# A hybrid decoder layer on one core: reciprocal roots on a few rows instead of whole tiles, the last block's second scale inside the feed-forward stage, S5 operators fetched a step sooner, the sample softmax placed later

## The chip, the cores and the metric

One NeuronCore of a Trainium2 chip runs the whole program: TensorE (PE, with its weight loads shown apart as PEld), VectorE (DVE), ScalarE (ACT), GpSimd (POOL), and one queue of SyncE (SP) from which every DMA is issued. The metric is device microseconds for one execution, median of several runs; less is better.

## The reference

One inference step of one decoder layer (width 1024) for a prompt of 2048 tokens and for 8 single-token samples that share all weights. Cut to what matters:

```python
h = rmsnorm(x)
[u_ssm | u_pool | q_mem | gate_logits] = h @ w_in
o_ssm  = S5 state-space branch of u_ssm, GELU, GLU
o_pool = trailing means of u_pool (windows 2,4,8,16), mapped per group, scaled
o_mem  = 4-head cross-attention from q_mem into 256 memory tokens
merged = sum_b sigmoid(gate_b) * (o_b @ w_branch_up[b])
x = x + rmsnorm(merged @ w_out)
x = x + rmsnorm(SwiGLU(rmsnorm(x)))
# rmsnorm(x) = x * rsqrt(mean(x*x) + eps) * g, in float32
```

The samples attend into caches of their own: 8 samples x 4 heads x 256 keys of 128, read from HBM.

## The kernel before

All tensors lie transposed, channels on the partitions and tokens on the free axis. Float32 accuracy comes from splitting every operand into a high part (ACT, L171) and a rest (DVE or POOL, L172) and adding three matmuls, hi*hi, hi*lo and lo*hi (`mmk`, L117). Those into the six PSUM tiles `pa` are called main matmuls here; transposes (L120) and small products go to the two tiles `pb`.

The prompt is cut into four blocks q = 0 to 3 of 512 tokens; block 1 (`QS`) carries the 8 samples too and is 520 wide, cut into 256 and 264. The mix stage runs over the blocks: `ssm_project`, `projections` and `gates` for the three branches in the order of a table, `out_project`, and `residual`. Then comes the feed-forward stage in two halves (`ffn_in`, with Strassen's seven products over sums of block pairs that `sums` computes and stores in `d_S`, loaded as tiles `S`) and `ffn_out`.

Work that is not main matmuls is written as generators in a list `background`; main code calls `step()` between its matmuls and so draws one piece of the list at a time, and `flush()` draws all that is left. The compiler's scheduler then fixes one order of instructions for each engine. Every engine executes its own order strictly, so a matmul that waits holds all matmuls behind it, and a DMA issue on SP that waits for a free buffer holds all issues behind it. `yield` is the place where a generator hands back; an empty `yield` pushes the rest of it one piece later.

The pieces that the change touches:

- A scale. `rsqrt_mean` sums squares over channels with one matmul against a tile of ones (every partition of the result holds the same row of 512 sums), and then computes 1/sqrt by a bit trick and three Newton steps on the full 128 x 512 tile: 11 DVE operations (L354, L342, L343, three times L345 to L347). It is used 11 times: `norm_stats` (blocks 1 to 3) and twice in each `residual`.
- `rsqrt_quick` (already used elsewhere: first norm, memory norm, finish) puts the sums into 4 columns of 128 tokens (5 of 104 in block 1) with matmuls of one column (`pb<-ones,tmp` in the trace), does the same steps on 128 x 4 (12 DVE operations, L367 to L373), and spreads the result back: one DVE multiply of the identity per column (L380), one 128-wide matmul against ones per column (`pb<-tmp,ones`), one ACT copy (L390).
- `residual(q)`: first scale; for each of 8 channel tiles a DVE multiply (L1253), a POOL add (L1254), a store, an ACT square (L1257), a DVE add into `st2` (L1259); then the second scale from `st2`, stored to `d_rb2`, which only `sums` reads. `residual(3)` runs alone, after all mix work and before the feed-forward stage.
- `s5_group(q, g)`: per block four groups. Operators `op(0..6)` are loaded from `d_ops` (L798) into six buffers `ops`; `op(2..4)` serve the matmuls of its last step.
- `sample_attention` (in block 1): per sample a broadcast load of the query (L1102), two loads of keys (L1106), POOL multiplies (L1107) and DVE reductions to scores `sc` (L1108), all through four buffers `xr`; two PE transposes of `sc` (L1110) start the softmax; its result goes to `d_ps`, and 16 steps with the values follow the same way (L1127 to L1132).

Of the kernel before, what the change touches and what calls it, by code (L numbers as in the profile page):

```python
# [13 lines left out]
I32 = mybir.dt.int32  # L14
# [3 lines left out]
MUL, ADD, SUB = ALU.mult, ALU.add, ALU.subtract  # L18
# [110 lines left out]
def trunk(ctx, tc, nc, I, O):  # L129
# [7 lines left out]
            "ev": 4, "S": 56, "f": 52, "z": 8}  # L137
    SIZE = {"tmp": 528, "ops": 512, "G": 512, "wr": 1024, "wh": 1024, "wl": 1024, "wt": 1024,
            "ev": HW_, "S": HW_, "f": HW_, "z": HW_}
    COMMON = ("xr", "tmp", "rb", "wr", "wh", "wl")  # L140
    stage = [None]

    def nm(tag):
# [3 lines left out]
    def slot(tag, dt=F32):  # L147
        n = nm(tag)
        p = base if tag in COMMON else stage[0]
        return p.tile([P, SIZE.get(tag, W520)], dt, tag=tag, name=n, bufs=BUFS[tag])  # L150
# [9 lines left out]
    def psum2():  # L160
        n = nm("pb")
        return psp.tile([P, 512], F32, tag="pb", name=n, bufs=2)
# [11 lines left out]
    def blocks(q):  # L174
        return [(0, 256), (256, 264)] if q == QS else [(0, 512)]

    def width(q):
        return W520 if q == QS else TQ
# [158 lines left out]
    def each(q, ps):  # L337
        return [(p_[:, :n], slice(o, o + n)) for p_, (o, n) in zip(ps, blocks(q))]

    def rsqrt_core(d, v, n):  # L340
        a = slot("tmp")[:, :n]
        V.tensor_scalar(d.bitcast(I32), v.bitcast(I32), -0.5, float(0x5F3759DF), MUL, ADD)  # L342
        V.tensor_scalar(v, v, -0.5, None, MUL)  # L343
        for _ in range(3):
            V.tensor_tensor(a, d, d, MUL)  # L345
            V.tensor_tensor(a, a, v, MUL)
            V.scalar_tensor_tensor(d, a, 1.5, d, ADD, MUL)  # L347

    def rsqrt_mean(dst, sums, bl):
        v = slot("tmp")  # L350
        for o, n in bl:
            ps = psum2()
            T.matmul(ps[:, :n], lhsT=ones, rhs=sums[:, o:o + n], start=True, stop=True)
            V.tensor_scalar(v[:, o:o + n], ps[:, :n], 1.0 / DM, EPS, MUL, ADD)  # L354
        sl = slice(bl[0][0], bl[-1][0] + bl[-1][1])
        rsqrt_core(dst[:, sl], v[:, sl], sl.stop - sl.start)

    def rsqrt_rows(sums, bl):
        lo, hi = bl[0][0], bl[-1][0] + bl[-1][1]
        ns = next(i for i in range(-(-(hi - lo) // P), 99) if (hi - lo) % i == 0)  # L360
# [31 lines left out]
    def rsqrt_quick(dst, sums, bl):  # L392
        rows = rsqrt_rows(sums, bl)
        spread(rows, bl[0][0], dst)
        return rows
# [35 lines left out]
    def norm_stats(q):  # L431
        n = width(q)
        st = slot("tmp")
        for k in range(KD):
            xt = load_x(q, k)
            if k == 0:
                S.activation(st[:, :n], xt[:, :n], AF.Square)
            else:
                sq = slot("tmp")
                S.activation(sq[:, :n], xt[:, :n], AF.Square)  # L440
                G.tensor_tensor(st[:, :n], st[:, :n], sq[:, :n], ADD)
            if k % 2:
                yield
        rb = slot("rb")
        rsqrt_mean(rb, st, blocks(q))
        nc.sync.dma_start(d_rb[q, :, :n], rb[:, :n])
        yield

# [346 lines left out]
    def s5_group(q, g, U, us, out):  # L795
        def op(i):
            t = slot("ops")
            nc.sync.dma_start(t, d_ops[g, i])  # L798
            return t

        Bre, Bim = op(0), op(1)
        pu = psum2()
        for i in range(4):
            T.transpose(pu[:, i * P:(i + 1) * P], U[:, i * P:(i + 1) * P], ident)
        Ut = slot("U")
        S.activation(Ut[:, :512], pu, AF.Copy)
        yield
        e = []
        for B in (Bre, Bim):
            pe = psum2()  # L810
            for i in range(4):
                sl = slice(i * P, (i + 1) * P)
                T.matmul(pe[:, sl], lhsT=B[:, sl], rhs=Ut[:, sl], start=True, stop=True)
            e.append(pe)
        if q == QS:
            samp = sample_state(g, us, Bre, Bim)
        Cs, Sn = op(5), op(6)
        Gr, Gi = slot("G"), slot("G")
        gr, gi = Gr[:, :512], Gi[:, :512]
        t0, t1 = slot("tmp")[:, :512], slot("tmp")[:, :512]  # L820
        V.tensor_tensor(gr, Cs, e[0], MUL)
        V.tensor_tensor(t1, Sn, e[0], MUL)
        V.tensor_tensor(t0, Sn, e[1], MUL)
        V.tensor_tensor(gi, Cs, e[1], MUL)
        G.tensor_tensor(gr, gr, t0, ADD)
        G.tensor_tensor(gi, gi, t1, SUB)
        yield
        for i in range(4):
            r = 4 * g + i
            sl = slice(i * P, (i + 1) * P)  # L830
            dec = r4[:, r:r + 1].to_broadcast([P, P])
            V.tensor_tensor_scan(gr[:, sl], dec, gr[:, sl], carry[0][:, r:r + 1], MUL, ADD)
            V.tensor_tensor_scan(gi[:, sl], dec, gi[:, sl], carry[1][:, r:r + 1], MUL, ADD)
        yield
        t2, t3 = slot("tmp")[:, :512], slot("tmp")[:, :512]
        t0, t1 = slot("tmp")[:, :512], slot("tmp")[:, :512]
        V.tensor_tensor(t0, gr, Cs, MUL)
        V.tensor_tensor(t1, gi, Sn, MUL)
        V.tensor_tensor(t2, gr, Sn, MUL)
        V.tensor_tensor(t3, gi, Cs, MUL)  # L840
        yield
        v3 = lambda a: a.rearrange("p (r n) -> p r n", r=4)
        gs = slice(4 * g, 4 * g + 4)
        for dst, a, b, o, cy in ((gr, t0, t1, SUB, carry[0]), (gi, t2, t3, ADD, carry[1])):
            V.tensor_copy(v3(dst)[:, :, 0], cy[:, gs])
            V.tensor_tensor(v3(dst)[:, :, 1:P], v3(a)[:, :, 0:P - 1], v3(b)[:, :, 0:P - 1], o)
            V.tensor_tensor(cy[:, gs], v3(a)[:, :, P - 1], v3(b)[:, :, P - 1], o)
        Tp, Wre, Wim = op(2), op(3), op(4)
        yield
        py = psum2()  # L850
        pyv = py.rearrange("p (t r x) -> p r t x", t=4, r=4)
        t3d = lambda a: a.rearrange("p (t x) -> p t x", t=4)
        for i in range(4):
            sl = slice(i * P, (i + 1) * P)
            T.matmul(pyv[:, i], lhsT=Ut[:, sl], rhs=t3d(Tp[:, sl]), start=True, stop=False)
            T.matmul(pyv[:, i], lhsT=gr[:, sl], rhs=t3d(Wre[:, sl]), start=False, stop=False)
            T.matmul(pyv[:, i], lhsT=gi[:, sl], rhs=t3d(Wim[:, sl]), start=False, stop=True)
        y = slot("tmp")[:, :512]
        gelu(y, py)
        if q == QS:  # L860
            ysT = sample_out(g, samp, Tp, Wre, Wim)
        yield
        pt = psum2()
        for t in range(4):
            T.transpose(pt[:, t * P:(t + 1) * P], y[:, t * P:(t + 1) * P], ident)
        yT = slot("U")
        S.activation(yT[:, :TQ], pt, AF.Copy)
        if q == QS:
            V.tensor_copy(yT[:, TQ:W520], ysT)
        out.append(yT)  # L870
        yield
# [220 lines left out]
    def sample_attention(qs, o_mem):  # L1092
# [7 lines left out]
        for b in range(NS):  # L1100
            qb = slot("xr")
            nc.sync.dma_start(qb[:, :512].rearrange("p (h d) -> p h d", h=NH),  # L1102
                              qv[b].unsqueeze(0).to_broadcast([P, NH, P]))
            for mt in range(2):
                kc = slot("xr")
                nc.sync.dma_start(kc[:, :512], I["ck"][b, mt])  # L1106
                G.tensor_tensor(kc[:, :512], kc[:, :512], qb[:, :512], MUL)  # L1107
                V.tensor_reduce(sc[:, mt, b, :], kc[:, :512].rearrange("p (h d) -> p h d", h=NH), AX, ADD)  # L1108
            yield
        pp = psum2()  # L1110
        for mt in range(2):
            T.transpose(pp[:NH * NS, mt * P:(mt + 1) * P], sc[:, mt].rearrange("p b h -> p (b h)"), ident)
# [5 lines left out]
        V.reciprocal(mx[:, 2:3], mx[:, 1:2])  # L1118
        V.tensor_scalar(e, e, mx[:, 2:3], None, MUL)
        nc.sync.dma_start(d_ps, e)  # L1120
        yield
        os_ = small([P, NS, NH], "os")
        dv = d_ps.rearrange("(b h) m -> b h m", b=NS)
        for b in range(NS):
# [119 lines left out]
    def residual(q, z, st):  # L1244
        n = width(q)
        rb = slot("rb")
        rsqrt_mean(rb, st, blocks(q))
        st2 = slot("rb2")
        yield
        for k in range(KD):  # L1250
            xt = load_x(q, k)
            zk = z[k][:, :n]
            V.tensor_tensor(zk, zk, rb[:, :n], MUL)  # L1253
            G.tensor_tensor(zk, zk, xt[:, :n], ADD)  # L1254
            nc.sync.dma_start(d_x2[q, k, :, :n], zk)
            sq = st2 if k == 0 else slot("tmp")
            S.activation(sq[:, :n], zk, AF.Square)  # L1257
            if k > 0:
                V.tensor_tensor(st2[:, :n], st2[:, :n], sq[:, :n], ADD)  # L1259
            yield  # L1260
        rb = slot("rb")
        rsqrt_mean(rb, st2, blocks(q))
        nc.sync.dma_start(d_rb2[q, :, :n], rb[:, :n])
        yield

    def own(q):
# [251 lines left out]
    for sb in range(len(SB)):  # L1518
        with tc.high_priority(offset=LEAD if sb == 0 else 0):
            prefetch()  # L1520
            got = left(sb)
        if sb + 1 < len(SB):
            background.append(sums(sb + 1))
        ffn_in(sb, got)
        flush()
# [115 lines left out]
```

## Time and profile before

| | |
|---|---|
| median of 3 runs | 3181.82 us (3180.26 to 3183.82) |
| profiled execution | 3181.19 us, of which span 3179.4 us |
| mean granted TensorE clock | 0.968 of full speed |
| busy: PE, DVE, ACT, POOL | 94%, 60%, 38%, 23% of the span |

Read it so: PE is busy nearly all the time, and the kernel ends when PE has worked through its order. What any edit can win is time in which PE stands still or runs at a lower granted clock, and this must be looked up place by place, as the shares are means over stages with different limits.

### The profile page before, as it was taken

How to read it: one execution, taken by the hardware profiler on the slowest of the kernel's cores; microseconds unless marked ns; L12 is line 12 of the kernel's file. 1: busy time of each engine (PE TensorE's matmuls, PEld its weight loads, DVE VectorE, ACT ScalarE, POOL GpSimd, SP SyncE). 2: the span in 40 equal slices, each digit the busy share in tenths (PEclk: the TensorE clock that was granted, in tenths of full speed). 3: DMA queues.
4: the chain of work that ended last, by engine and by line, in shares of the span. 5: the costliest groups of instructions: out<-in, count | busy, mean ns of one | idle time of the engine just before them, and what ended most of it. 6: DMA issues, size and time to landing. Idle time of an engine off the chain costs nothing. (4 is left out here: it accounts for less than half of the span.)

```text
span 3179.4 us, 51273 instructions
## 1 busy us (share of the span) xinstructions
PE 2993.8 (94%) x20319; PEld 2758.2 (87%) x20319; DVE 1914.7 (60%) x3143; ACT 1206.6 (38%) x2091; POOL 745.3 (23%) x630
## 2 busy tenths in 40 slices
PE   7989998599998999989995999999999999999997
PEld 6778877499997788868884999999999998999997
DVE  7876748574538655496466855557555554445364
ACT  4532434322344334443333433335333334434343
POOL 2564244442245122450212000000000000011012
PEclk9989998789999999989997999999999999999999
DMA  6344333662334333344273742225322225445575
GB/s 215 109 163 133 120 120 108 167 205 86 123 118 154 124 100 125 126 156 150 90 229 118 241 123 81 81 81 158 96 80 81 80 79 171 147 159 165 159 254 171
DMA packets 205728, 432.99 MB, mean 136 GB/s; under 512 B 47472, under 2 KB 55216, under 8 KB 205488
## 3 DMA queue, kind: packets, MB, share of 16 engines
q1 hardware_dynamic: 205488, 429.72, 42.8%
q8 instruction: 159, 2.61, 0.3%
q14 instruction: 81, 0.66, 0.1%
HBM read 362.82 MB, written 66.49 MB: 135 GB/s over the span
## 5 line engine op out<-in xcount | busy, mean ns | idle before, releaser
L117 PE MATMUL pa<-S,wh 128*128 128x258 f32 (+1 forms) x4928 | 889.5, 283 | 11.8 <-ACT S L171 5.6
L171 ACT ACTIVATE wh<-wr 128x1024 fp32r<-128x1024 f32 (+1 forms) x460 | 458.3, 997 | 1023.4 <-PE pa L117 778.8
L117 PEld LDWEIGHTS pa<-S,wh 128*128 128x128 f32 x4928 | 759.6, 189 | 15.6 <-ACT S L171 7.1
L117 PE MATMUL pa<-S,wl 128*128 128x258 f32 (+1 forms) x2464 | 691.6, 282 | 0.0
L117 PE MATMUL pa<-h,wh 128*128 128x512 f32 (+2 forms) x2560 | 673.6, 358 | 15.7 <-ACT tmp L1055 7.9
L172 DVE TENSOR_TENSOR wl<-wr,wh 128x1024 fp32r<-128x1024 f32 x372 | 437.6, 1178 | 389.9 <-ACT wh L171 377.7
L117 PEld LDWEIGHTS pa<-h,wh 128*128 128x128 f32 x2560 | 440.7, 193 | 85.5 <-ACT tmp L1055 8.3
L117 PE MATMUL pa<-br,wh 128*128 128x512 f32 (+2 forms) x1848 | 475.3, 353 | 22.4 <-ACT wh L171 9.0
L117 PE MATMUL pa<-f,wh 128*128 128x258 f32 (+1 forms) x2816 | 469.1, 283 | 7.2 <-ACT f L171 4.3
L117 PEld LDWEIGHTS pa<-S,wl 128*128 128x128 f32 x2464 | 467.9, 190 | 0.0
L117 PE MATMUL pa<-h,wl 128*128 128x512 f32 (+2 forms) x1280 | 420.3, 357 | 0.0
L117 PEld LDWEIGHTS pa<-f,wh 128*128 128x128 f32 x2816 | 400.2, 190 | 9.6 <-ACT f L171 5.6
L117 PEld LDWEIGHTS pa<-br,wh 128*128 128x128 f32 x1848 | 312.7, 191 | 71.2 <-ACT wh L171 9.0
L172 POOL TENSOR_TENSOR wl<-wr,wh 128x1024 fp32r<-128x1024 f32 (+1 forms) x88 | 214.9, 2443 | 438.3 <-ACT wh L171 332.3
L117 PE MATMUL pa<-f,wl 128*128 128x258 f32 (+1 forms) x1408 | 312.2, 283 | 4.6 <-DVE wl L172 4.6
L117 PE MATMUL pa<-br,wl 128*128 128x512 f32 (+2 forms) x924 | 296.9, 352 | 0.9 <-DVE wl L172 0.9
L117 PEld LDWEIGHTS pa<-h,wl 128*128 128x128 f32 x1280 | 232.5, 193 | 34.4 <-issue 0.5
L1373 POOL TENSOR_TENSOR tmp<-tmp,ev 128x516 f32<-128x516 f32 (+1 forms) x44 | 58.4, 1326 | 848.2 <-ACT tmp L1372 848.2
L172 DVE TENSOR_TENSOR wl<-wt,wh 128x1024 fp32r<-128x1024 f32 x88 | 108.0, 1228 | 224.0 <-ACT wh L171 224.0
L117 PEld LDWEIGHTS pa<-f,wl 128*128 128x128 f32 x1408 | 230.5, 190 | 4.8 <-DVE wl L172 4.8
L117 PEld LDWEIGHTS pa<-br,wl 128*128 128x128 f32 x924 | 164.7, 191 | 24.5 <-DVE wl L172 1.3
L1347 ACT ACTIVATE ev<-pa 128x258 f32<-128x258 f32 (+1 forms) x264 | 100.6, 384 | 197.7 <-PE pa L117 178.8
(335 smaller groups left out, 3515.6 us busy)
## 6 DMA issues: line engine op xcount, KB each, us to landing
wr<-in_w_all SPq DMA_DIRECT2D x408, 512.0 KB, 3.5
ops<-d_ops SPq DMA_DIRECT2D x112, 256.0 KB, 3.5
xr<-in_x_t SPq DMA_DIRECT2D x80, 256.0 KB, 3.6
xr<-d_x SPq DMA_DIRECT2D x72, 256.0 KB, 4.2
wr<-in_w_all SPq DMA_DIRECT2D x40, 384.0 KB, 3.3
d_f<-tmp SPq DMA_DIRECT2D x44, 258.0 KB, 4.2
xr<-d_f SPq DMA_DIRECT2D x44, 258.0 KB, 3.7
d_f<-tmp SPq DMA_DIRECT2D x44, 256.0 KB, 4.2
```

Source lines behind the costliest of these rows:

```text
L117: self._done(self.nc.tensor.matmul(*a, **k))
L171: S.activation(dst_hi, src, AF.Copy)
L172: (eng or V).tensor_tensor(dst_lo, src, f(dst_hi), SUB)
L1347: both(lambda u, s: S.activation(dst[:, s], X[u][:, :w], AF.Copy))
L1373: G.tensor_tensor(f0[:, :n], f0[:, :n], p1[:, :n], MUL)
```

## The change

It has four parts. All 11 uses of `rsqrt_mean` become `rsqrt_quick`. The second scale of a residual becomes a generator of its own; for blocks 0 to 2 it still follows at once, for block 3 it becomes the first background work of the first `ffn_in`, and the buffer `rb2` moves to the pool that all stages share (`COMMON`). In `s5_group` the loads `op(2..4)` are issued one step sooner. In `sample_attention` six empty yields stand ahead of the softmax and three more behind the store of its result.

```diff
-    COMMON = ("xr", "tmp", "rb", "wr", "wh", "wl")
+    COMMON = ("xr", "tmp", "rb", "rb2", "wr", "wh", "wl")
...
     def norm_stats(q):
...
-        rsqrt_mean(rb, st, blocks(q))
+        rsqrt_quick(rb, st, blocks(q))
...
     def s5_group(q, g, U, us, out):
...
             V.tensor_tensor_scan(gi[:, sl], dec, gi[:, sl], carry[1][:, r:r + 1], MUL, ADD)
+        Tp, Wre, Wim = op(2), op(3), op(4)
         yield
...
-        Tp, Wre, Wim = op(2), op(3), op(4)
         yield
         py = psum2()
...
     def sample_attention(qs, o_mem):
...
+        for _ in range(6):
+            yield
         pp = psum2()
...
         nc.sync.dma_start(d_ps, e)
-        yield
+        for _ in range(4):
+            yield
...
     def residual(q, z, st):
...
-        rsqrt_mean(rb, st, blocks(q))
+        rsqrt_quick(rb, st, blocks(q))
...
+        sums2[q] = st2
+        if q + 1 < NQ:
+            yield from second_scale(q)
+    sums2 = {}
+    def second_scale(q):
         rb = slot("rb")
-        rsqrt_mean(rb, st2, blocks(q))
-        nc.sync.dma_start(d_rb2[q, :, :n], rb[:, :n])
+        rsqrt_quick(rb, sums2[q], blocks(q))
+        nc.sync.dma_start(d_rb2[q, :, :width(q)], rb[:, :width(q)])
         yield
...
         if sb + 1 < len(SB):
+            background.append(second_scale(NQ - 1))
             background.append(sums(sb + 1))
         ffn_in(sb, got)
```

How the order of the engines changes, at three places. Line numbers of the changed kernel differ: its L349 to L355, L362, L780, L1084, L1088, L1238 and L1244 are L367 to L373, L380, L798, L1102, L1106, L1253 and L1259 of before.

PE in block 1, before: the transposes of the scores `sc` stand behind main matmul 2268 of the program and ahead of the pool branch's products (`pb<-br`).

```order
L117 MATMUL pa_5769<-h_4274,wl_5559 128x256
L117 MATMUL pa_5770<-h_4274,wl_5559 128x264
L120 MATMUL pb_5524<-ident_63,sc_5026 32x128
L120 MATMUL pb_5542<-ident_63,tmp_5404 128x128 x4
L120 MATMUL pb_5524<-ident_63,sc_5026 32x128
L117 MATMUL pb_5562<-br_5145,wh_5067 128x256
```

PE in the changed kernel: the pool branch's products and two small S5 products (`sut`) of the next group come first, and the transposes stand behind main matmul 2358.

```order
L117 MATMUL pa_6032<-h_4244,wl_5765 128x256
L117 MATMUL pa_6033<-h_4244,wl_5765 128x264
L117 MATMUL pb_5884<-sut_5880,ops_5681 128x8 x4
L117 MATMUL pb_5884<-sut_5880,ops_5683 128x8 x4
L120 MATMUL pb_5918<-ident_63,sc_5067 32x128 x2
L117 MATMUL pa_6032<-h_4289,wh_5764 128x256
```

So 90 main matmuls and the pool products moved ahead of the transposes.

SP in block 1, before: `ops_5365`, `ops_5367` and `ops_5369` are `op(2..4)` of group 0, the first two behind three key loads (two of them not shown), the third behind six.

```order
L1106 DMA xr_5039<-in_ck 128x512
L798 DMA ops_5365<-d_ops 128x512
L798 DMA ops_5367<-d_ops 128x512
L1106 DMA xr_5043<-in_ck 128x512
L1001 DMA hs_5502<-in_sp_t 128x8x15
L1102 DMA xr_5055<-d_qs 128x4x128
L1106 DMA xr_5057<-in_ck 128x512
L1106 DMA xr_5061<-in_ck 128x512
L290 DMA wr_5819<-in_w_all 128x1024
L1102 DMA xr_5210<-d_qs 128x4x128
L798 DMA ops_5369<-d_ops 128x512
```

SP in the changed kernel, where they are `ops_5096`, `ops_5098` and `ops_5100`:

```order
L780 DMA ops_5096<-d_ops 128x512
L1079 DMA d_qs<-qrow_5064 32x128
L780 DMA ops_5098<-d_ops 128x512
L290 DMA wr_5706<-in_w_all 128x1024
L1084 DMA xr_5068<-d_qs 128x4x128
L1088 DMA xr_5070<-in_ck 128x512
L1088 DMA xr_5074<-in_ck 128x512
L1084 DMA xr_5078<-d_qs 128x4x128
L780 DMA ops_5100<-d_ops 128x512
L985 DMA out_sp<-hs_5366 128x8x15
L1088 DMA xr_5080<-in_ck 128x512
```

Two of the three stand ahead of all key loads now, the third behind two of them.

DVE where the feed-forward stage begins, before (L354 and L342 belong to the second scale of block 3, L265 to L267 to weight sums, L172 to `S` tiles):

```order
L1259 TENSOR_TENSOR rb_2847_15262<-rb_2847_15262,tmp_15322 128x512
L354 TENSOR_SCALAR tmp_15326<-pb_15327 128x512
L265 TENSOR_TENSOR wt_15353<-wr_15351,wr_15349 128x512
L267 TENSOR_TENSOR wt_15354<-wr_15351 128x512
L342 TENSOR_SCALAR rb_15325<-tmp_15326 128x512
L172 TENSOR_TENSOR S_15404<-xr_15401,S_15403 128x516
L266 TENSOR_TENSOR wt_15353<-wr_15351,wt_15353 128x512
L172 TENSOR_TENSOR S_15410<-xr_15407,S_15409 128x516
L343 TENSOR_SCALAR tmp_15326<-tmp_15326 128x512
```

DVE there in the changed kernel:

```order
L1244 TENSOR_TENSOR rb_2857_15398<-rb_2857_15398,tmp_15458 128x512
L265 TENSOR_TENSOR wt_15471<-wr_15469,wr_15467 128x512
L267 TENSOR_TENSOR wt_15472<-wr_15469 128x512
L172 TENSOR_TENSOR S_15522<-xr_15519,S_15521 128x516
L266 TENSOR_TENSOR wt_15471<-wr_15469,wt_15471 128x512
L172 TENSOR_TENSOR S_15528<-xr_15525,S_15527 128x516
```

No operation of the second scale is left between the last L1259 and the first `S` tiles; its 12 small ones come 23 rows later.

## Rows read from the trace of the kernel before

**Rows 1.** The page, busy time of each engine:

```profile
PE 2993.8 (94%) x20319; PEld 2758.2 (87%) x20319; DVE 1914.7 (60%) x3143; ACT 1206.6 (38%) x2091; POOL 745.3 (23%) x630
```

**Rows 2.** PE's waits by releaser: total us, times, longest us.

```profile
PE pb L117 <- DVE rb L1259: 26.9, 1, 26.9
PE pb L120 <- DVE sc L1108: 19.5, 1, 19.5
PE pa L117 <- ACT tmp L1055: 7.9, 2, 7.6
```

**Rows 3.** Four stretches: length; busy us of PE, PEld, DVE, ACT, POOL; clock, DMA.

```profile
480.00:680.00 200.00, 144.76 (x1005) 134.68 (x1005) 140.89 (x251) 65.22 (x144) 92.88 (x76) 0.80 0.55 153
960.00:1050.00 90.00, 77.71 (x361) 62.91 (x360) 82.39 (x128) 42.33 (x88) 49.36 (x37) 0.94 0.44 145
1360.00:1430.00 70.00, 57.24 (x256) 46.17 (x256) 65.83 (x96) 33.12 (x70) 42.24 (x35) 0.88 0.54 173
1690.00:1780.00 90.00, 50.28 (x309) 44.09 (x308) 72.86 (x102) 34.93 (x61) 14.62 (x9) 0.79 0.53 165
```

**Rows 4.** Timeline of PE in block 1: start, us, instruction, idle before it.

```profile
574.02 0.59 PE L117 MATMUL pb<-ops,U 128*128 128x128 f32 x2 [4.17 <-DMA ops<-d_ops]
...
587.54 0.80 PE L117 MATMUL pb<-ops,G 128*128 128x128 f32 x2 [5.79 <-DMA ops<-d_ops]
...
624.47 0.37 PE L120 MATMUL pb<-ident,sc 128*32 128x128 f32 x1 [19.48 <-DVE sc L1108]
```

**Rows 5.** Line L1108, a wait of L1107 (us, times), line L1132: ns, first and last start.

```profile
L1108 DVE TENSOR_REDUCE sc<-xr x16: 671/686/686, 567.1 to 624.9; 128x4 f32<-128x512 f32 x16
...
  DMA xr<-in_ck: 30.2, 8
...
L1132 DVE TENSOR_REDUCE os<-xr x16: 670/686/689, 636.5 to 690.6; 128x2 f32<-128x512 f32 x16
```

**Rows 6.** Timelines of DVE, PE and POOL where the feed-forward stage begins.

```profile
1699.13 0.69 DVE L1241 TENSOR_TENSOR tmp<-tmp,tmp 128x512 f32<-128x512 f32 x1 [4.87 <-ACT tmp L1238]
1701.10 0.69 DVE L354 TENSOR_SCALAR tmp<-pb 128x512 f32<-128x512 f32 x1 [1.28 <-PE pb L117]
...
1709.15 11.31 DVE L1253 TENSOR_TENSOR acc<-acc,rb 128x512 f32<-128x512 f32 x8
...
1732.16 0.69 DVE L172 TENSOR_TENSOR S<-xr,S 128x516 fp32r<-128x516 f32 x1
...
1699.97 1.10 PE L117 MATMUL pb<-tmp,ones 128*128 128x512 f32 x2 [1.50 <-DVE tmp L1241]
1727.93 2.04 PE L117 MATMUL pb<-rb,ones 128*128 128x512 f32 x2 [26.87 <-DVE rb L1259]
...
1709.92 13.33 POOL L1254 TENSOR_TENSOR acc<-acc,xr 128x512 f32<-128x512 f32 x8 [30.34 <-DVE acc L1253]
```

**Rows 7.** Timelines of existing quick scales: last two columns, six columns, four columns.

```profile
3162.24 0.58 PE L117 MATMUL pb<-ones,tmp 128*128 128x1 f32 x4 [1.02 <-DVE tmp L1412]
3162.85 0.16 DVE L367 TENSOR_SCALAR rsq<-pb 128x2 f32<-128x2 f32 x1 [0.76 <-PE pb L117]
...
3165.08 0.48 DVE L380 TENSOR_SCALAR tmp<-ident,rsq 128x128 f32<-128x128 f32 x2
...
3165.51 1.19 PE L117 MATMUL pb<-tmp,ones 128*128 128x128 f32 x4 [2.70 <-DVE tmp L380]
...
2786.39 1.01 PE L117 MATMUL pb<-ones,tmp 128*86 128x1 f32 x12
...
77.18 1.05 PE L117 MATMUL pb<-tmp,ones 128*128 128x128 f32 x8
```

**Rows 8.** Line L390, and a timeline of POOL and DVE at 73 us.

```profile
L390 ACT ACTIVATE rb<-pb x7: 237/529/722, 24.5 to 3049.7; 128x512 f32<-128x512 f32 x2, 128x430 f32<-128x430 f32 x2, 128x86 f32<-128x86 f32 x2, 128x256 f32<-128x256 f32 x1
...
73.16 2.40 POOL L172 TENSOR_TENSOR wl<-wr,wh 128x1024 fp32r<-128x1024 f32 x1 [7.82 <-ACT wh L171]
73.23 2.36 DVE L372 TENSOR_TENSOR rsq<-rsq 128x4 f32<-128x4 f32 x1
```

More of the change, by code (lines that the diff above doesn't have):

```diff
@@ L338, in each @@
         return [(p_[:, :n], slice(o, o + n)) for p_, (o, n) in zip(ps, blocks(q))]
[L340 to L356, printed above, removed]
     def rsqrt_rows(sums, bl):
```

## Prediction

> **What bounds the kernel now.** I read the page first. PE is busy 94% of the span [rows 1]; DVE comes next with 60%. So the end is set by PE's own order, and 6% of 3179.4 us, some 186 us, is time in which PE has nothing to do. Then I read PE's waits by releaser, and asked which of them the diff can reach. The three longest shown [rows 2] are all near it: 26.9 us in one piece for L1259, the sum of squares in `residual`; 19.5 us in one piece for the scores of the samples; 7.6 us for an attention row that a busy DVE delivers late (L1055 is ACT's, fed by DVE). Last I measured the four stretches in which residuals and samples run [rows 3]. Block 1 (480 to 680 us) has 200 - 144.76 = 55.2 us of idle PE, at a mean granted clock of 0.80. The same places in blocks 2 and 3 have 12.3 and 12.8 us, and DVE is busy 82.39 of 90 and 65.83 of 70 us there, so DVE sets the pace. The start of the feed-forward stage (1690 to 1780) has 39.7 us.
>
> **The start of the feed-forward stage.** Before, the last sum of squares of the first scale ends at 1699.13 + 0.69 = 1699.82, and L1253 starts at 1709.15: 9.33 us, of which DVE computes from 1701.10 on [rows 6]. The quick form in the tail [rows 7] takes, for two columns, 3162.85 to 3165.08 = 2.23 us for its 12 small operations, 0.48 us for two L380, and its spread starts at 3165.51, 2.66 us after the first small operation. For four columns I add two more L380 (0.5), the rest of a spread (some 1.0) and an ACT copy (0.53 for 512 columns [rows 8]). From 1701.10, where L354 starts, that is 2.66 + 0.5 + 1.0 + 0.53 = 4.7, about 1705.8 with 0.3 us to hand over at 1706.1. So L1253 starts 3.0 us sooner. The middle stays: eight additions on POOL take 13.33 us in all from 1709.92 on [rows 6], and L1253 itself is drawn out by them to 11.31 us for 8. This is why most of the 26.9 us will remain. Behind it, PE gets the ones matmul of the second scale at 1727.93, right when L1259 is done; the first `S` rest is made only at 1732.16, because an evaluation (L354), L265, L267 and L342 stand ahead of it and because DVE waits for PE first. In the changed order only L265 and L267 (0.6 us each) do, and the first is at 1729.1: 3.1 us sooner. The remaining ten operations of the old second scale (6.6 us) stood between `S` tiles on a busy DVE (72.86 of 90 us [rows 3], the start of it spent waiting); they become 12 x 0.19 + 4 x 0.24 = 3.2 us, later. Of the 3.4 us I count 2. Sum: -3.0 - 3.1 - 2 = -8, bounds -5 and -10.
>
> **Block 1.** Two waits for S5 operators, 4.17 us at 574.02 and 5.79 us at 587.54 [rows 4], belong to `op(2..4)` of group 0. In the changed order two of these loads stand ahead of all loads of keys and one behind two, so both waits go: -10.0. The wait for the scores, 19.48 us, ends at 624.47, when the last of 16 L1108 has run (624.9 [rows 5]). The transposes that waited now come 90 main matmuls and the pool products later. PE came to them at 624.47 - 19.48 = 605. The 90 matmuls at 144.76/1005 = 0.14 us [rows 3] and 24 pool products at 0.3 (0.59 for two [rows 4]) are 20 us, and waits between them make it more, so PE now comes at 625 or later, when the chain is done. So -19.5. Of the 7.6 us for L1055 [rows 2] I take 5, since the first scale ahead of it occupies DVE for 8.05 us (1701.10 to 1709.15 [rows 6] is the same work) and now for 3.2. That is 34.5 us. Not all of it stays won: the work that moves ahead needs DVE too (140.89 of 200 us [rows 3]), the six last L1108 are interleaved with its evictions, and POOL waits 30.2 us for keys [rows 5], which a DMA queue that starts them later does not shorten. I give back a quarter: -26. The bounds are -10, only the operators, and -45, above.
>
> A rule of clocks matters for that upper bound. In block 1 the 144.76 us of busy PE ran at a mean of 0.80 of 2.4 GHz, that is, much of it at the 1.2 GHz level right behind the waits [rows 3]; at 1.00 they would be 144.76 x 0.80 = 115.8 us, 29 us less. If a third of this came back with the waits, 34.5 + 10 = 45. I leave it out of the sum, as blocks 2 and 3 with gaps of a few us show 0.94 and 0.88 still. The Trainium skill, "TensorE: Matmul & The Clock Gate", Part 1, says that the throttled clock is the default and that activity releases it; by that rule alone removing waits returns the clock as well, and block 1 would give 45 rather than 26. The trace agrees as far as 0.79 and 0.80 stand at the two stretches with the longest waits.
>
> **Blocks 2 and 3.** Four scales there are on a saturated DVE. Each falls from 8.05 us to 3.2, -4.9, together 19 us of DVE. At most the 25 us in which PE is idle there can shrink, and PE idles only at the ends of chains. I take -7, bounds 0 and -16. The three scales of `norm_stats` lie where PE is ahead; nothing.
>
> **What it costs.** PE does more. Six one-column sums take 0.87 us net (1.01 less the overlap [rows 7]), so four take 0.6, and a spread of four about 0.9 (1.05 less overlap); a 512-wide ones matmul took 1.10 at the mixed clock [rows 6], some 0.9 at full. That is +0.6 per scale, ten scales where PE is the bound: +6. The ACT copy (0.53, 11 times) is hidden by an ACT that is busy 38% [rows 1]. The later values chain of the samples (L1132 from 636.5 to 690.6 [rows 5]) is 54 us long; PE never waits for it among the waits shown, and with main work some 30 us ahead and a chain that starts about as before, I count nothing, and make it a rival.
>
> **Sum.** -8 - 26 - 7 + 6 = -35 us. From the profiled execution's own 3181.19 us (1.79 us outside its span) that is 3146; the median of the runs shown is 0.6 us higher, which I neglect. A measurement of this kernel can tell about 0.2%, 6.4 us, from no change.
>
> **The rivals.** (a) *The keys set the pace anyway*: the chain L1106, L1107, L1108 takes 58 us (567.1 to 624.9 [rows 5]) through four buffers, and PE, freed of the transposes, waits instead for evictions and adds that DVE delivers behind L1108 in its order. For it speaks the 30.2 us of POOL waiting for keys; against it that 16 L1108 are only 11 us of DVE. Or the values now come late for the memory branch, with the same price. Block 1 then gives 10: -8 - 10 - 7 + 6 = -19, 3162. (b) *The clock comes back too*: block 1 gives 45 and blocks 2 and 3 up to 10: -8 - 45 - 10 + 6 = -57, 3124. (c) *PE waits for DVE where it never did* (slower). Before, only DVE waited for the ones matmul; a scale's product went to DVE and nothing came back to PE. Now PE's strict order holds a spread that needs 12 + 4 operations of DVE. From sums to spread the tail takes 3.3 us (3162.24 to 3165.51) with an idle DVE. Where DVE has a backlog, say four operations of 0.7 us, it is 6. If the ten scales outside the boundary cost PE 3.5 us each, the 35 us are gone; from 4.2 us on the kernel is measurably slower, and at 5 it ends at 3196. One thing makes such a backlog worse: a 128 x 4 operation of this form took 2.36 us instead of 0.16, exactly while a POOL operation of 2.40 us ran [rows 8]. Of 21 such L372 one was hit. By that rate it is well under one hit, 2.2 us, for each chain of 9 operations that read two tiles: 0.4 x 2.2 x 10 = 9 us on DVE, on PE only where the cover is short. The Trainium skill, "SBUF — State Buffer", section "Who interferes with whom", says that DVE and GpSimd share a pair of ports as an exclusive lock held for a whole instruction; by that rule the small operations lose their smallness whenever POOL is at work, and by one hit in each chain the scales would cost 22 us of DVE more. The trace agrees, with 2.36 us beside 2.40. Against (c) speaks that the order puts 26 to 55 main matmuls between sums and spread at nine of the ten places (13 at one, in block 1), 4 to 12 us at 0.14 (144.76/1005) to 0.22 us (77.71/361 [rows 3]) each.
>
> **How the numbers follow.** My forecast (3132 to 3158): 0.52. (a) 0.24; (b) 0.12; (c) 0.12, of which 0.07 is measurably slower and 0.04 within 0.2%. From (a), 0.01 falls within 0.2% as well. So faster 0.88, same 0.05, slower 0.07. The likeliest gives 3146; the range that leaves out a tenth at either end runs from 3116, near the bounds -10, -45, -10 with +0 for PE, to 3170, beyond (a).
>
> **What would show it.** Right: no wait of PE for `sc` over 3 us and none for `ops`; the wait for L1259 about 23 to 24 us instead of 26.9; the first `S` rest 6 us nearer to the last L1241; DVE busy some 20 us less in blocks 2 and 3 together with less idle PE; a clock of block 1 above 0.80. Wrong: long waits of PE on L380 (c), waits for L1018, L1219 or L172 in block 1 that add up to 20 us (a), or a new wait of the memory branch near its values.

## The result, and the profile after

The changed kernel takes 3144.73 us (median of four, 3140.58 to 3146.45), beside 3181.04 for the kernel before: ratio 0.9883, interval 0.9866 to 0.9900. That is 36 us less. On the chip of the last group of experiments it was 3137.31 beside 3176.07, ratio 0.9879. The profiled execution has a span of 3144.5 us and a mean clock of 0.975.

PE's waits by releaser in the changed kernel (total us, times, longest us):

```profile
PE pa L117 <- ACT S L171: 20.1, 4, 16.0
...
PE pa L117 <- ACT tmp L1037: 7.7, 3, 7.4
PE pb L117 <- DVE tmp L362: 6.8, 3, 2.7
...
PE pb L120 <- DVE ops L172: 5.5, 3, 4.2
...
PE pb L117 <- DVE ysT L916: 4.6, 1, 4.6
```

Against [rows 2] the reader sees four things. The wait for the scores is gone. The one for an attention row (L1055, now L1037) has stayed: 7.4 us instead of 7.6. The long wait at the feed-forward stage is no longer one for the second scale's sums but for the first `S` tile that ACT makes, and it is 16.0 us instead of 26.9. And PE waits for spreads (L362) in three places only.

The stretches of [rows 3] in the changed kernel, cut so that each holds the same main matmuls as before. Between the first and the second stands what follows in block 1:

```profile
481.00:650.10 169.10, 137.90 (x1033) 130.39 (x1032) 114.89 (x243) 66.42 (x146) 79.63 (x65) 0.88 0.50 147
650.10:770.80 120.70, 113.62 (x942) 111.77 (x941) 73.94 (x148) 31.53 (x58) 40.36 (x30) 0.96 0.50 163
942.80:1028.20 85.40, 77.94 (x386) 62.77 (x386) 71.75 (x136) 43.86 (x92) 45.17 (x37) 0.98 0.45 152
1338.00:1403.90 65.90, 58.05 (x274) 45.40 (x273) 55.56 (x100) 35.73 (x75) 34.71 (x30) 0.96 0.51 173
1664.60:1748.30 83.70, 53.82 (x337) 49.18 (x335) 62.85 (x110) 35.64 (x63) 15.00 (x9) 0.78 0.58 177
```

The kernel of before in the second of them:

```profile
680.10:789.20 109.10, 109.10 (x942) 107.24 (x941) 61.02 (x132) 31.52 (x58) 22.66 (x19) 1.00 0.38 127
```

Idle PE falls from 55.2 to 31.2 us in the first part of block 1, from 12.3 to 7.5 and from 12.8 to 7.9 in blocks 2 and 3, and from 39.7 to 29.9 at the start of the feed-forward stage. DVE's busy time in blocks 2 and 3 falls by 10.6 and 10.3 us, together the 20 that the prediction named as a sign. The clock of the first part of block 1 rises from 0.80 to 0.88. But the rest of block 1, in which PE had no idle time at all, becomes 11.6 us longer: 7.1 us of it are idle time, and as many PE instructions (942) take 113.6 us instead of 109.1 at a clock of 0.96 instead of 1.00.

To see where time went I took the start of each main matmul (into `pa`; 18948 in every trace) and compared equal counts. The first column of numbers is the time of the stretch before, the others what it became, in us. "Again" is a second profile of the changed kernel, e9; the experiments are described below; 6600 to 7200, which changes by 0.1 at most, is left out.

| main matmuls | before | changed | again | e1 | e2 | e3 | e4 | e5 | e11 |
|---|---|---|---|---|---|---|---|---|---|
| to 1800 | 483.9 | +1.1 | +1.3 | +2.1 | -2.9 | -2.1 | -1.0 | -2.8 | +1.3 |
| 1800 to 3200, block 1 | 296.4 | -19.4 | -26.0 | -1.1 | -1.3 | +1.6 | -10.2 | -15.5 | -6.9 |
| of it 1800 to 2460 | 187.2 | -30.9 | -32.1 | -8.6 | -4.7 | -1.0 | -21.2 | -27.1 | -6.9 |
| of it 2460 to 3200 | 109.1 | +11.5 | +6.1 | +7.5 | +3.4 | +2.7 | +11.0 | +11.6 | +0.1 |
| 3200 to 6600, blocks 2 and 3 | 736.3 | -7.2 | -9.9 | -9.3 | -0.9 | -1.4 | +0.2 | -0.2 | -8.9 |
| 7200 to 8200, start of feed-forward | 184.6 | -6.7 | -5.6 | -0.1 | -2.8 | +2.9 | +0.2 | +1.5 | -6.6 |
| 8200 to the end | 1308.6 | -2.9 | -3.7 | -3.1 | -5.1 | -3.8 | -1.8 | -2.1 | -2.9 |

The last row is 2 to 5 us in all kernels of the table, also in those that change nothing there, so the likely reason is a profiled execution of before that was a little slow at the end. The scatter of a single stretch shows in the others: e3 and e5 have +2.9 and +1.5 at the feed-forward stage, whose instructions they do not touch. "Changed" and "again" are one kernel, and differ by 1.2 us up to main matmul 2460 and by 5.4 from there to 3200. Differences under 3 us in one cell say nothing, and in that part of block 1 not under 6.

### The profile page after: what moved, and what is told of

The parts are those of the page before. It is cut to its first block, busy times and chain, and to the rows that moved or that the text cites. A ratio compares the mean times of both kernels' runs of the same rounds, so it can differ in the third digit from the quotient of the medians.

```text
span 3144.5 us, 51655 instructions
## 1 busy us (share of the span) xinstructions
PE 2996.9 (95%) x20479; PEld 2764.9 (88%) x20479; DVE 1858.3 (59%) x3187; ACT 1214.7 (39%) x2105; POOL 741.6 (24%) x630
## 4 chain that ended last, share of the span: by engine, by line
PE 82%; DVE 5%; DMA 5%; issue 3%; POOL 2%; ACT 2%; SPq 1%; DVEq 0%; POOLq 0%; ACTq 0%
PE pa L117 78%; PE pb L117 3%; DMA xr<-d_f 1%; DVE wl L172 1%; PE pb L120 1%; DMA xr<-in_ck 1%; DMA xr<-d_S 1%; DVE acc L1238 1%; DMA xr<-in_cv_t 0%; ACT wh L171 0%; SPq L679 0%; DMA ops<-d_ops 0%; POOL acc L1239 0%; DMA xr<-d_qs 0%; DVE G L815 0%
## 5 line engine op out<-in xcount | busy, mean ns | idle before, releaser
L117 PEld LDWEIGHTS pa<-S,wh 128*128 128x128 f32 x4928 | 762.5, 190 | 29.4 <-ACT S L171 21.4
L117 PE MATMUL pa<-h,wh 128*128 128x512 f32 (+2 forms) x2560 | 667.2, 356 | 19.5 <-ACT tmp L1037 7.4
L172 DVE TENSOR_TENSOR wl<-wr,wh 128x1024 fp32r<-128x1024 f32 x372 | 434.2, 1169 | 393.5 <-ACT wh L171 380.8
L172 POOL TENSOR_TENSOR wl<-wr,wh 128x1024 fp32r<-128x1024 f32 (+1 forms) x88 | 214.2, 2436 | 442.2 <-ACT wh L171 392.5
L172 DVE TENSOR_TENSOR wl<-wt,wh 128x1024 fp32r<-128x1024 f32 x88 | 108.1, 1228 | 223.5 <-ACT wh L171 223.5
```

The costliest lines, as they stand in the source:

```text
L117: self._done(self.nc.tensor.matmul(*a, **k))
L172: (eng or V).tensor_tensor(dst_lo, src, f(dst_hi), SUB)
```

## The experiments

The theory that I took from the prediction: each part works at its own place (scores and operators in block 1, scales in blocks 2 and 3, the second scale at the feed-forward stage). The main rival: relief of DVE by the small scales is the source of nearly all, in block 1 too. Four kernels made one part of the change each.

**e1, the scales alone.**

```diff
-        rsqrt_mean(rb, st, blocks(q))
+        rsqrt_quick(rb, st, blocks(q))
```

(in `residual`; the same for `st2` there, and in `norm_stats`.) 

> Kernel of before with the quick scales alone. Theory A (each part works in its own place): block 1 gains little, 0 to 4 us, because its long waits are for scores and operators; blocks 2 and 3 gain the 4 to 8 us seen after the full change, the start of the feed-forward stage 3 to 5; sum -11 us, 3170. Theory B (DVE relief is the source of nearly all): the scores' chain ends sooner too and the long wait shrinks by half; sum -25 us or more, 3156.

3165.71 us beside 3178.48; ratio 0.9958 (0.9945 to 0.9970), -13 us. By place it is the theory's: -9.3 in blocks 2 and 3, nearly nothing in block 1, where PE's idle time stays at 55 us in all. The waits by releaser show the scores still in the way, 14.0 us instead of 19.5, and the saved part is spent waiting on other DVE work:

```profile
PE pb L117 <- DVE rb L1259: 19.4, 1, 19.4
PE pb L120 <- DVE sc L1108: 14.0, 1, 14.0
PE pb L117 <- DVE tmp L380: 9.5, 4, 2.7
PE pb L117 <- DMA ops<-d_ops: 8.9, 4, 5.5
...
PE pa L117 <- DVE br L172: 8.8, 2, 7.8
```

The rival falls in block 1. At the feed-forward stage I expected -3 to -5 and found -0.1: there both scales stand at the boundary, and the second one's round trip (19.4 us until its sums can start, then 2.7 us for its L380) still stands ahead of the first `S` tiles.

**e2, the second scale moved, nothing else** (it stays on full tiles; the generator `second_scale` and the pool of `rb2` as in the change, not shown again).

```diff
+            background.append(second_scale(NQ - 1))
             background.append(sums(sb + 1))
```

> Kernel of before with the last block's second scale in the feed-forward stage (still on full tiles) and rb2 in the common pool, nothing else. Theory A: the first S rest no longer has L354 and L342 and a wait for PE ahead of it, and ACT can make S tiles earlier: -3 to -6 us at the start of the feed-forward stage, 3176 to 3178. Theory B: that start is paced by POOL's eight additions and by loads, -1 or less.

3173.91 us, 0.9983 (0.9974 to 0.9992), -5 us. The gain in time is clear of noise; that it arises at its place is less so, as -2.8 there is no more than the scatter. The profiles have -0.1 at that boundary for e1, -2.8 for e2 and -5.6 to -6.7 where both are in.

**e3, the operators alone.**

```diff
+        Tp, Wre, Wim = op(2), op(3), op(4)
         yield
         t2, t3 = slot("tmp")[:, :512], slot("tmp")[:, :512]
...
-        Tp, Wre, Wim = op(2), op(3), op(4)
         yield
```

Between the old place and the new one stand two `yield`s, so the loads are issued two pieces of the list sooner, not one as the section on the change has it. 

> Kernel of before with the three operators loaded a step sooner, nothing else. Theory A: PE's waits of 4.2 and 5.8 us for them in block 1 go; but the wait for scores behind them ends where the key loads let it, so that the scores' wait grows by as much: -2 to +2 us in all. Theory B: the ten us stay won, -10.

3179.10 us, 1.0001 (0.9993 to 1.0010): nothing, as the theory said. PE's waits show why:

```profile
PE pb L120 <- DVE sc L1108: 21.3, 1, 21.3
...
PE pa L117 <- DVE br L172: 8.7, 2, 5.0
```

The waits for `ops` are gone from the list, and the wait for the scores is 21.3 us instead of 19.5; other waits on DVE take the rest. PE comes sooner to the chain of the scores, and waits there for longer.

**e4, the later softmax alone** (six empty yields ahead of it, three more behind). 

> Kernel of before with the later softmax, nothing else. Theory A: the 19.5 us wait goes, and the waits for operators stay; about half of the won time returns as waits for evictions and for later S5 groups, -8 to -14 us. Theory B: without DVE relief the wait only moves to other instructions, -4 or less.

3165.89 us, 0.9954 (0.9940 to 0.9968), -14.6 us by the ratio and -12.6 by the medians. The 19.5 us are gone, and what stays is

```profile
PE pb L117 <- DMA ops<-d_ops: 10.4, 2, 6.1
...
PE pb L117 <- DVE br L1018: 9.0, 3, 6.8
```

the operators, now in the open, and evictions of the pool branch that queue on DVE behind an L1108 which waits for POOL: the kind of wait that rival (a) named. The row on DVE just ahead of the L1018 that PE waits 6.8 us for:

```profile
620.49 0.69 DVE L1108 TENSOR_REDUCE sc<-xr 128x4 f32<-128x512 f32 x1 [6.58 <-POOL xr L1107]
```

**e5, softmax and operators together.** 

> Kernel of before with the later softmax and the earlier operators, without the quick scales and the second scale moved. Theory A: the ten us of the operators count as soon as no wait for scores stands behind them, so the two give more than their sum (0 and -14): -18 to -22 us, about 3158. Theory B: they add up, -14, 3165.

3160.31 us, 0.9943 (0.9931 to 0.9955), -18 us. That is 3 to 5 more than softmax alone, and the first part of block 1, where the operators are, went from -21.2 to -27.1 (e3: -1.0). The intervals of e4 and e5 overlap, so that the operators count only behind a later softmax is what the profiles say, and the times alone do not settle it.

**e11, the changed kernel with the softmax where it was** (the nine yields taken out). 

> Changed kernel with the sample softmax where it was (nine empty yields taken out). Theory A: the wait for scores is back at some 15 us, as with the quick scales alone, but later S5 groups no longer are pushed back; 10 to 15 us slower than the changed kernel. Theory B: with scales and operators out of the way the scores' chain ends so much sooner that little of the wait is left: 0 to 5 us slower.

3156.16 us beside 3137.31 of the changed kernel (e9) on the same chip; ratios to before 0.9935 (0.9922 to 0.9947) and 0.9879 (0.9864 to 0.9894). So the softmax's place is worth 19 us once everything else is in, and 15 alone, a difference that the intervals do not rule out as noise. It is more than I expected: the wait is not 15 but

```profile
PE pb L120 <- DVE sc L1090: 21.1, 1, 21.1
```

long, since PE, freed of the operators and with quicker scales, arrives sooner. The table shows that the 19 us are a net figure: the later softmax gains 24 to 25 us up to main matmul 2460 (-6.9 without it, -30.9 and -32.1 with it) and gives back 6 to 11 behind that (+0.1 without, +11.5 and +6.1 with). 

> The changed kernel itself, run beside the next three on one chip, so that they can be compared with it. Its time should stand to that of before as it did, 0.988.

 That held: 0.9879.

The four parts alone add up to -0.42 - 0.17 + 0.01 - 0.46 = -1.04%, 33 us; together they give 1.17 to 1.21%, 37 to 38 us. The 4 to 5 us between are within what the five intervals allow, so that the parts help each other is not shown by the times; the places where it would be are the operators behind the softmax (e5) and the boundary of the two stages.

The next group asks what paces the parts that did not shrink: the feed-forward boundary, and the 7.4 us for L1037.

**e6, additions of the last block's residual on DVE; e7, every second one.**

```diff
-            G.tensor_tensor(zk, zk, xt[:, :n], ADD)
+            (V if q + 1 == NQ else G).tensor_tensor(zk, zk, xt[:, :n], ADD)
```

(e7: `q + 1 == NQ and k % 2`.) 

> Changed kernel, with the eight additions of the last block's residual on DVE instead of POOL. Theory A: POOL's additions, in turn with DVE's multiplies, pace the start of the feed-forward stage (18.6 us from the first multiply to the last sum of squares); on DVE alone it is 23 operations of 0.69 = 15.9: -2.7 us, 3142. Theory B: the squares on ACT or the loads pace it: 0.

 

> Changed kernel, with every second addition of the last block's residual on DVE. If DVE and POOL hold each other up for whole operations: 20 operations of 0.69 on DVE and four of POOL in turn, about 17 us instead of 18.6, -1 to -2. If they run side by side: 8 multiplies and 4 additions on DVE are 8.3 us, with sums 13: -5.

3137.27 us, 0.9877 (0.9864 to 0.9890), and 3141.86 us, 0.9888 (0.9875 to 0.9901). Neither differs from the changed kernel's 0.9879 to 0.9883 by more than its interval. The timelines answer all the same. DVE in e6, then POOL in e7:

```profile
1672.38 4.91 DVE L1238 TENSOR_TENSOR acc<-acc,rb 128x512 f32<-128x512 f32 x8 [2.27 <-ACT rb L372]
...
1685.44 1.44 DVE L1239 TENSOR_TENSOR acc<-acc,xr 128x512 f32<-128x512 f32 x2 [1.83 <-DMA xr<-in_x_t]
```

```profile
1676.18 1.64 POOL L1239 TENSOR_TENSOR acc<-acc,xr 128x512 f32<-128x512 f32 x1 [27.54 <-DVE acc L1238]
...
1690.62 1.26 POOL L1239 TENSOR_TENSOR acc<-acc,xr 128x512 f32<-128x512 f32 x1 [7.66 <-DMA xr<-in_x_t]
```

Without POOL, eight multiplies take 4.91 us; with POOL's additions in turn 11.31. And an addition of POOL takes 1.64 us beside DVE and 1.26 alone. So the two engines do hold each other up, as I had read from [rows 8]. But when that brake is taken off, the next one stands close behind: L1239 waits for x, which comes through the four buffers `xr` that the additions free. From the first multiply to the last sum of squares it is 18.6 us in the changed kernel, 17.2 in e6 (15.9 expected) and 18.7 in e7 (17 or 13 expected).

**e8, the sums of the last block's second scale on PE.** One-column matmuls of each squared tile are accumulated over the eight tiles, so that the seven DVE additions are not made (cut to the place of the sums; `rsqrt_rows` then takes them as they are).

```diff
+            if q + 1 == NQ:
+                for i in range(4):
+                    T.matmul(pe_sum[0][:, i:i + 1], lhsT=sq[:, i * P:(i + 1) * P], rhs=ones[:, 0:1],
+                             start=k == 0 and i == 0, stop=k == KD - 1 and i == 3)
-            if k > 0:
+            elif k > 0:
                 V.tensor_tensor(st2[:, :n], st2[:, :n], sq[:, :n], ADD)
```

> Changed kernel, with the second scale's sums over channels of the last block accumulated by one-column matmuls on the idle PE, so that the seven DVE additions L1244 (7.4 us) are gone there. Theory A: those additions stand between POOL's last addition and the first S rest: the S rest comes about 4.5 us sooner and the time falls by 4 to 5, 3140. Theory B: loads of S tiles and ACT's copies for them pace that start: -2 or less.

3135.99 us, 0.9873 (0.9859 to 0.9888). The first `S` rest starts 22.4 us behind the last L1226 (which ends at 1668.42) where the changed kernel has 26.7; that is 4.3 us sooner, where 4.5 was expected. The row in e8:

```profile
1690.80 0.69 DVE L172 TENSOR_TENSOR S<-xr,S 128x516 fp32r<-128x516 f32 x1 [0.67 <-ACT S L171]
```

It waits for ACT now. By stretches 2 to 3 us remain (-8.5 at 7200 to 8200, beside -6.7 and -5.6), which is the scatter of that cell; in the time it cannot be told from nothing.

**e10, additions of block 0's residual on DVE** (the edit of e6 with `q == 0`). 

> Changed kernel, with the eight additions of block 0's residual on DVE instead of POOL. Theory A: the wait of 7.4 us for L1037 stayed because its row maximum L1033 stands in DVE's order behind eight multiplies L1238 that POOL's additions stretch from 0.69 to 1.4 us each; without POOL they take 0.69, the wait falls to 1 to 4 us, and the time by 2 to 5. Theory B: the table load and the rows ahead of it on ACT make that wait; it stays over 7 us, and DVE, loaded with 5.5 us more, loses 0 to 4.

3139.49 us, 0.9878 (0.9864 to 0.9891), no change in the time; the wait in question fell from 7.37 to 4.16 us. The DVE rows of the changed kernel, and then of e10, with the row maximum's scaling L1033 that L1037 needs:

```profile
497.98 5.36 DVE L1238 TENSOR_TENSOR acc<-acc,rb 128x512 f32<-128x512 f32 x4
...
503.86 6.19 DVE L1238 TENSOR_TENSOR acc<-acc,rb 128x512 f32<-128x512 f32 x4
509.97 1.29 DVE L1033 TENSOR_SCALAR mx<-mx 128x2 f32<-128x2 f32 x2
```

```profile
495.46 3.19 DVE L1238 TENSOR_TENSOR acc<-acc,rb 128x512 f32<-128x512 f32 x4
...
499.18 2.49 DVE L1238 TENSOR_TENSOR acc<-acc,rb 128x512 f32<-128x512 f32 x4
501.58 0.16 DVE L1033 TENSOR_SCALAR mx<-mx 128x2 f32<-128x2 f32 x1
```

In both, eight multiplies stand ahead of L1033. With POOL in turn they take 11.6 us, without 5.7. So the cause that theory A named is right, though the wait ends at 4.16 us and not between 1 and 4, and the gain of 2 to 5 us in the time did not come. What takes it back no run shows; that DVE has eight more operations to do is the likely reason.

**e12, the edits of e6, e8 and e10 together.** 

> Changed kernel with all that seemed to gain: one-column sums on PE for the last block's second scale, and the additions of the first and the last block's residual on DVE. If the gains add up, 6 to 10 us faster than the changed kernel; if the loads of x through four buffers set the pace at the feed-forward stage, 3 to 5.

3133.88 us, 0.9865 (0.9850 to 0.9881), beside 3137.31 and 0.9879 (0.9864 to 0.9894) of the changed kernel in the same group. The lowest median of all; but the intervals overlap, and that it beats the changed kernel is not shown.

## Why the prediction was right, and where only its sum was

The sum was forecast as -35 and is -36 in the medians, -34.7 in the two profiled executions. By its steps:

**Block 1: -26 forecast, -19.4 and -26.0 in two profiles.** The long wait went, as said, and the transposes stood clear of the chain: the last L1090 starts at 621.8 and PE comes to them at 634.0 without waiting. The operators' waits went too (in block 1 none of the 10.0 us is left), but e3 shows that the step which priced them was wrong in kind: by themselves those 10 us are worth nothing, because the wait for the scores stood behind them on the same engine and took them over. They are a gain only together with the later softmax.

The step that failed outright is the 5 us for the attention row. I put the lateness of L1055 down to the operations of the old scale (twelve with L354, not eleven). The rows of before say otherwise: DVE had scaled the row maximum by 500.44, before PE began to wait at 503.0, and L1055 stood in ACT's order behind squares L1257 that waited for POOL's additions, and behind a table load of 1.28 us.

```profile
500.29 0.15 DVE L1051 TENSOR_SCALAR mx<-mx 128x2 f32<-128x2 f32 x1
...
507.64 0.63 ACT L1257 ACTIVATE tmp<-acc 128x512 f32<-128x512 f32 x1 [1.04 <-POOL acc L1254]
508.27 1.28 ACT L1055 ACT_TABLE_LOAD   x1
...
510.64 0.80 PE L117 MATMUL pa<-h,wh 128*128 128x256 f32 x2 [7.62 <-ACT tmp L1055]
```

In the changed kernel the wait has nearly the same length, 7.37 us, from another cause: the scheduler put L1033 behind eight L1238, which POOL stretches (e10), and ACT waits for it:

```profile
511.23 0.47 ACT L1037 ACTIVATE tmp<-pa,mx 128x256 f32<-128x256 f32 x1 [3.29 <-DVE mx L1033]
```

A second step failed: the later values chain, which I had counted at nothing. PE never waits for its results. But DVE executes its reductions L1117 in order with the S5 steps, and an L1117 that waits for POOL holds the S5 step that PE needs. In the changed kernel (the matmuls whose result L803 reads had ended by 669.8):

```profile
671.86 0.69 DVE L1117 TENSOR_REDUCE os<-xr 128x2 f32<-128x512 f32 x1 [3.59 <-POOL xr L1116]
673.91 0.69 DVE L1117 TENSOR_REDUCE os<-xr 128x2 f32<-128x512 f32 x1 [1.37 <-POOL xr L1116]
674.52 0.68 DVE L803 TENSOR_TENSOR G<-ops,pb 128x512 f32<-128x512 f32 x1
...
677.07 0.39 PE L120 MATMUL pb<-ident,tmp 8*128 8x8 f32 x4 [2.86 <-DVE tmp L804]
```

Three waits of PE for S5 steps, 7.1 us (4.7 in the second profile), lie in main matmuls 2460 to 3200; two of them stand behind a waiting L1117. That part of block 1 takes 11.5 and 6.1 us more than before, and in e11, which differs by the softmax's place alone, 0.1 more. (e1 has 4.7 us of idle PE there with the softmax in its old place, so a later chain is not the only way to it.)

The quarter given back, 8.6 us, was thus too small: of the 29.4 us of waits for scores and operators, 12.6 came back as idle time elsewhere in block 1 (11.9 in the second profile). Of these the waits that rival (a) listed rose only from 7.8 to 12.5 us (L1018, now L1000, and L172), as PE's timeline shows in part:

```profile
569.53 0.69 PE L120 MATMUL pb<-ident,tmp 128*128 128x128 f32 x2 [4.15 <-DVE ops L172]
...
604.69 0.58 PE L117 MATMUL pb<-br,wh 128*128 128x256 f32 x1 [4.57 <-DVE ysT L916]
...
611.90 0.58 PE L117 MATMUL pb<-br,wh 128*128 128x256 f32 x1 [2.29 <-DVE br L1000]
```

The rest of the difference between the two profiles is the clock: PE's idle time in block 1 is 38.3 and 37.6 us, its busy time 2.6 and 8.6 us less than before.

**Blocks 2 and 3, and the cost on PE: -7 and +6 forecast, -7.2 and -9.9 measured in blocks 2 and 3.** The +6 was for ten scales, six of which lie in these blocks, so the forecast for the stretch is -3.4. The cost was sized too large. Where PE is the bound and one scale of `norm_stats` lies (main matmuls 3200 to 4400), the table's kernels with quick scales have +0.9 us, more than my 0.6. But only the three scales of `norm_stats` lie so (the others up to 1800, and from 5200 to 5800, with +0.3 in the changed kernel). The rest lie where PE had idle time; I charged ten. That the extra matmuls cost nothing there is argued, as no run has them without the relief of DVE.

**Start of the feed-forward stage: -8 forecast, -6.7 and -5.6 measured.** The mechanism was right. The rows of the changed kernel that answer [rows 6]:

```profile
1673.51 0.69 DVE L1226 TENSOR_TENSOR tmp<-tmp,tmp 128x512 f32<-128x512 f32 x1 [4.87 <-ACT tmp L1223]
...
1681.16 11.31 DVE L1238 TENSOR_TENSOR acc<-acc,rb 128x512 f32<-128x512 f32 x8 [2.27 <-ACT rb L372]
...
1700.91 0.69 DVE L172 TENSOR_TENSOR S<-xr,S 128x516 fp32r<-128x516 f32 x1
...
1674.35 1.38 PE L117 MATMUL pb<-ones,tmp 128*128 128x1 f32 x8 [1.50 <-DVE tmp L1226]
1678.44 2.05 PE L117 MATMUL pb<-tmp,ones 128*128 128x128 f32 x8 [2.72 <-DVE tmp L362]
1696.50 0.80 PE L117 MATMUL pa<-S,wh 128*128 128x258 f32 x2 [16.01 <-ACT S L171]
...
1701.66 0.58 PE L117 MATMUL pa<-S,wh 128*128 128x258 f32 x1 [4.36 <-DVE S L172]
```

From the last sum (1674.20) to L1238 it is 6.96 us instead of 9.33: 2.4 us won, where I said 3.0. The term was mis-sized by the spread, which takes 2.05 us here and not the 1.0 that I added for it. The first `S` rest starts 26.7 us behind that sum instead of 32.3, so 5.6 us sooner, where I said 6.1. Of the 2 us that I counted for the old operations between `S` tiles, 1.1 at most are left in one profile and nothing in the other. The middle, L1238 in 11.31 and POOL behind it, stayed to the hundredth. My sign "the wait for L1259 falls to 23 or 24 us" was wrong in its form: PE now does the spread in that time and then waits 16.01 and 4.36 us for `S`.

**The rivals.** (a) did not come true with its price, though its kinds of wait did in part, the values by way of DVE's order. (b) came in part, the clock of the first part of block 1 rising to 0.88. The Trainium skill, "TensorE: Matmul & The Clock Gate", Part 1, says that activity releases the throttled clock; the trace agrees, as with 31.2 us idle instead of 55.2 more of the time was at the 2.4 GHz level. At the start of the feed-forward stage, with still 29.9 us idle, it stayed at 0.78, beside 0.79 before. My 29 us for a full return of the clock took the stretch's mean of 0.80 for PE's busy time; the mean covers the idle time too, so they were an upper bound. (c), the slower one, cost 1.4 us: of PE's waits for L362 only one (1.42 us at 533.26, the place with 13 main matmuls of cover) is new in the mix stage, one lies at the boundary, and one is the tail's, which was there before. (The tenth place, the last block's second scale, has 72 main matmuls of cover, more than the 55 that I gave as the most.)

**The sum.** That it met so closely is in part luck. Block 1 came up to 6.6 us short and the feed-forward stage 1.3 to 2.4 short, blocks 2 and 3 gave 4 to 6 more than forecast, and some 3 us of both profiles lie in the last row, which no part of the change explains.

## What to carry to other kernels

Ask of every wait that an edit removes what the same engine waits for next: ten us of waits for data were worth nothing until the 20 us wait behind them was gone (e3, e5). Ask of work that an edit moves what stands next to it in the engine's order at the new place: the values chain, moved later, held S5 steps that PE needed (table, e11). Moving an instruction past work that does not need it, and making a chain of small operations out of full tiles, pays where the engine that executes it is behind, and costs little where enough independent work stands between the sums and their use; a dozen main matmuls was nearly enough here. And look at the pace of the pair of engines that share work, and at what stands behind it: at the boundary the eight rounds of DVE and POOL took 18.6 us, against 7.0 for the scale, and without POOL still 17.2 (e6).

## What the runs showed that I had not expected

The first small integer step L350, which reads one tile only, is held as well: in the changed kernel it takes 2.39 us at 489.78, beside a POOL operation on `wl` of 2.40 us that started at 489.74.

```profile
489.78 2.39 DVE L350 TENSOR_SCALAR rsq<-rsq 128x4 int32<-128x4 int32 x1
```

```profile
489.74 2.40 POOL L172 TENSOR_TENSOR wl<-wr,wh 128x1024 fp32r<-128x1024 f32 x1 [2.71 <-ACT wh L171]
```

Of the 198 small steps in the changed kernel (18 scales of 11 each, without the one that reads PSUM) three took over 0.3 us, each time L350, with 2.35 to 2.40 us beside a POOL operation on `wl`; in the second profile again three. That is 0.17 to a scale, where I priced 0.4, and none of the three is seen in a wait of PE for L362. My rate was one hit in 21 L372; by all 63 steps of before that read two tiles it would have been 0.14. The prediction counted only the nine operations of a chain that read two tiles as exposed, and in the changed kernel none of those was hit; these rows say that one with a single tile is exposed, too. The Trainium skill, "SBUF — State Buffer", section "SBUF: two separate sides", gives the lock to a DVE operation with two SBUF inputs or in a two-port mode; the trace agrees with the lock's length, 2.39 beside 2.40 us, and no run here shows in which mode L350 ran.
